# A hybrid attention layer on one core: four transfers a unit for sixteen, a product on VectorE, and other step counts

## The chip, the cores and the metric

The kernel runs on one core of a Trainium2 chip. The metric is the device time of one execution in microseconds. One execution is profiled, and the times below are those of its trace. The engines are TensorE (PE in the profile, and PEld for its weight loads), VectorE (DVE), ScalarE (ACT), GpSimd (POOL) and SyncE (SP), which issues the transfers.

## What is computed

One layer over 512 positions of width 1024 with two token mixers that read the same input: an attention of three branches (A) and a gated linear recurrence (B). Cut to what matters here:

```python
h = x @ w_in + b_in
(q_a, kv_a, g_nsa, z_a, q_b, f_b, i_b, z_b, gm_a, gm_b) = split(h)
# A: 8 heads in 2 groups of 4, width 64
o_cmp = masked_softmax(q @ kc.T) @ vc              # compressed keys and values
o_slc = masked_softmax(rope(q) @ rope(k_slc).T) @ v_slc
o_win = masked_softmax(rope(q) @ rope(k_win).T) @ v_win
o_a = (gt[0] * o_cmp + gt[1] * o_slc + gt[2] * o_win) * silu(z_a)
# B: recurrence over chunks of 64
o_b = hgrn2(q_b, f_b, i_b, lb)
o_b = o_b * rsqrt(mean(square(o_b)) + eps) * norm_g * silu(z_b)
y = sigmoid(gm_a) * (o_a @ w_branch_a) + sigmoid(gm_b) * (o_b @ w_branch_b)
out = layer_norm(alpha * x + y @ w_out)
```

With 512 positions the selected blocks and the window both cover all that comes before a position, so these two branches are causal attention with keys and values of their own.

## The kernel before

Everything is kept in SBUF with channels on the 128 partitions and positions along the row, up to the last stage. A product in float32 is done as three products of a high and a low part: `split2` casts the high part on ACT (L170) and subtracts it on DVE for the low part (L171). So each tile that goes into TensorE waits for a cast and then for a subtraction.

**What sets the order.** TensorE and the queue SP run what the program says in its order. The backbone is a row of projections: `proj(name)` does one 128-column tile of the input projection, 24 matmuls into one of two PSUM buffers `pa`; it loads the weights of the tile three further on and splits those of the tile two further on (`wraw`, `whi`, `wlo`, three buffers each). Into these projections other work is woven. A chain is a generator; every six matmuls of a projection (every second `kt`) make one tick (`weave.tick`, L82-94), at which each chain that is due runs on to its next `yield`. The number it yields is how many ticks it then rests. These numbers stand in the table `D` (L70-71): a chain `keys` that yields `D["r0"]` goes on r0 ticks later. A chain's instructions go into the queues of the engines at the tick at which it runs, so `D` sets what stands ahead of what on every engine.

**The chains.** `keys` and `queries` (r0) turn a projected tile by position and split it; `kh`, `kl` hold the keys of both branches. `cmp_kv` (c1, c2, c3) makes the compressed keys and values `kcB`, `vcB`, from a hidden tile that TensorE transposes into `hT`; `cmp_scores` and `cmp_probs` (p0, p1, p2) their softmax. `hgrn` (h0 to h6) is the recurrence, `hgrn_norm` (n0, n1, n2) its norm and gate, which makes the tiles `ob`.

**The units.** The masked attention runs in six units, `(i, branches)`: the last block of 128 queries (i = 3) with branch 0, then with branch 1, then i = 2 with either, then i = 1 with both and i = 0 with both. `attn_scores` (v0 to v3, e0) issues the score products of a unit, four of its eight heads at a time, then the masked reads with the row's minimum on DVE (L676) and the exponentials on ACT (L679). `soften` (e1, t0, t3, t1) scales the rows with gate and sum (L700 on ACT, L702 on DVE), and then turns the blocks: DVE transposes blocks of 32x32 into the one buffer `big` (L710), and transfers on SP bring these to their partitions in the one buffer `turn` (L719-721). After t1 ticks `values` splits the turned blocks (high part `t4<-turn` on ACT, low part in place on DVE) and after t2 more multiplies them with the values `vv` into two PSUM buffers `pso`. Since `turn` is one buffer, the next unit's transfers wait for this unit's values, and the next unit's transposes into `big` wait for this unit's transfers. With a query block's last product the sums go into `asum` (L747 on ACT, L751, L752 on DVE).

`attn_sum` (a5) adds the compressed branch, and when all four query blocks are there, multiplies with the gate (L781) and splits the four tiles `oa`.

**The end.** Eight groups of branch projections follow, four for mixer B with `ob` and then four for mixer A with `oa` (`BRANCH`, L922-950). Ahead of the first group of A, all chains are run to their end (`weave.drain`). Each group loads weights `wbr` three groups ahead, and output weights `wout` whose mean is taken out (L884, L886, L898, L899). A group's result is gated (L942), added to mixer B's (L946) and split, the tiles `y`. At the end come the output product and the norm by rows.

Of the kernel before, what the change touches and what calls it, by code (L numbers as in the profile page):

```python
# [13 lines left out]
ALU = mybir.AluOpType  # L14
# [6 lines left out]
NEG = -1.0e30  # L21
# [28 lines left out]
def _columns(name):  # L50

    c = np.arange(_COLS[name], _COLS[name] + 128)
    if name[0] == "q" and name[1] != "b" or name[:2] == "za":
# [12 lines left out]
K_ID, K_TRI, K_CM, K_RV, K_SM, K_COS, K_SIN, K_MASK, K_END = (  # L66
    0, 128, 256, 384, 388, 900, 1412, 1924, 2436)


D = dict(h0=6, h2=4, h3=7, h4=0, h5=5, h6=3, n0=6, n1=7, n2=4, c0=1, c1=5, c2=5, c3=4, r0=5, p0=5, p1=5, p2=2, s0=8,  # L70
         s2=5, s3=0, v0=10, v1=8, v2=7, v3=8, e0=4, e1=3, t0=6, t1=5, t2=4, t3=5, t4=1, a5=0)


class _Weave:
# [32 lines left out]
def layer_kernel(ctx: ExitStack, tc: tile.TileContext, xT, xn, w0, wi, wf, wv, small, brow, consts,  # L107
                 w1, w2, wbr, wout, lng, lnb, out):
    nc = tc.nc
    V, A, G = nc.vector, nc.scalar, nc.gpsimd  # L110
# [10 lines left out]
    def dma(o, i):  # L121
        tc.keep_in_program_order(nc.sync.dma_start(o, i))  # L122
# [3 lines left out]
    t2 = ctx.enter_context(tc.tile_pool(name="t2", bufs=57))  # L126
    t4 = ctx.enter_context(tc.tile_pool(name="t4", bufs=3))
# [8 lines left out]
    def T2(n=512, dt=F32):  # L136
        return t2.tile([P, n], dt, name="t2", tag="t2")
# [7 lines left out]
    def TURN():  # L145
        return turn.tile([P, 4096], F32R, name="turn", tag="turn")
# [7 lines left out]
    def PS():  # L154
        return pss.tile([P, 512], F32, name="pss", tag="pss")
# [4 lines left out]
    def PO():  # L160
        return pso.tile([P, 512], F32, name="pso", tag="pso")
# [4 lines left out]
    def act_set(name):  # L166
        return tc.keep_in_program_order(A.preload_act_table_set(name)).ins

    def split2(src, dst_hi, dst_lo):
        A.copy(dst_hi, src)  # L170
        V.tensor_tensor(dst_lo, src, dst_hi.bitcast(F32), ALU.subtract)  # L171
# [18 lines left out]
    for kt in range(KT):  # L190
# [6 lines left out]
        h, l, wh, wl = T2(dt=F32R), T2(dt=F32R), T2(dt=F32R), T2(dt=F32R)  # L197
# [160 lines left out]
    def chunks(ap):  # L358
        return ap.rearrange("p (t c s) -> p t c s", c=2, s=64)
# [28 lines left out]
    def hgrn(h):  # L388
# [11 lines left out]
        for w, e in ((1, e2), (0, e1)):  # L400
            V.tensor_tensor(chunks(e), cm[:, w].unsqueeze(3).to_broadcast([P, 4, 2, 64]), bc, ALU.subtract)
        yield D["h2"]
        qp = T2()
# [8 lines left out]
        V.tensor_tensor(e2, e2, k, ALU.mult)  # L412
        yield D["h3"]
        V.tensor_tensor(e1, e1, k, ALU.mult)
# [7 lines left out]
        V.tensor_tensor(qmc[:, :, 1], qpc[:, :, 1], ebc[:, :, 0, 63:64].to_broadcast([P, 4, 64]), ALU.mult)  # L422
        yield D["h4"]
        kMT = T2()
# [3 lines left out]
        for t in range(4):  # L428
# [4 lines left out]
                          pst_.rearrange("p (t s) -> p t s", s=128))  # L433
        yield D["h5"]
        while len(vi) < 4:
# [8 lines left out]
        for t in (1, 2):  # L444
            c = slice(128 * t, 128 * t + 128)
            V.scalar_tensor_tensor(st[:, c], st[:, 128 * t - 128:128 * t], dlab[:, t:t + 1], pu[:, c],
                                   ALU.mult, ALU.add)
        yield D["h6"]
        po = PO()
# [12 lines left out]
    def hgrn_norm():  # L462
        while len(osq) < 4:
            yield 1
        yield D["n0"]
        pm = PS()
        for h in range(4):
            T.matmul(pm[32 * h:32 * h + 32], ones, osq[h][1], start=True, stop=True)
        rs = T2()
        V.tensor_scalar(rs, pm, EPS, None, ALU.add)  # L470
        yield D["n1"]
        nat = act_set("natural_log_exp_and_others")
        with tc.issue_after(nat):
            A.activation(rs, rs, AF.Ln)
            A.activation(rs, rs, AF.Exp, scale=-0.5)
        exps.append(act_set("exp_and_others"))
        rms = []
        for h in range(4):
            rms.append(T2())
            for b in range(4):  # L480
                dma(rms[h][32 * b:32 * b + 32], rs[32 * h:32 * h + 32])
            yield 3
        yield D["n2"] - 9
        for h in range(4):
            while "zb%d" % h not in zs:
                yield 1
            o = osq[h][0]
            G.tensor_tensor(o, o, rms[h], ALU.mult)
            yield 2
            V.scalar_tensor_tensor(o, o, ngh[:, h:h + 1], zs["zb%d" % h], ALU.mult, ALU.mult)  # L490
            ob[h] = T2(dt=F32R), T2(dt=F32R)
            split2(o, *ob[h])
            yield 1
# [72 lines left out]
    def rope(raw):  # L566
        rot, r = T2(), T2()
        for b in range(4):
            dma(rot[32 * b:32 * b + 32], raw[32 * (b ^ 1):32 * (b ^ 1) + 32])
        V.tensor_tensor(r, raw, cosT, ALU.mult)  # L570
        return r, rot

    KH = cst.tile([P, 2, 512], F32R, name="kh")
    KL = cst.tile([P, 2, 512], F32R, name="kl")

    def keys(br, raw):
        r, rot = rope(raw)
        yield D["r0"]
        V.tensor_tensor(rot, rot, sinT, ALU.mult)
        V.tensor_tensor(r, r, rot, ALU.add)  # L580
        split2(r, KH[:, br], KL[:, br])
        ready.add("keys%d" % br)

    QAB = {}
# [60 lines left out]
    def attn_scores():  # L645
        blocks.append(BIG())
        for u, (i, brs) in enumerate(units):
            n, nb = 128 * (i + 1), len(brs)
            for ms in ((0, 1, 2, 3),) if i == 0 else ((0, 1), (2, 3)):
# [31 lines left out]

                weave.late.append(masked)
                weave.start(soften(u, ms, ts, den), D["e1"])
                yield D["v%d" % i]

    def soften(u, ms, ts, den):
        i, brs = units[u]
        n, nb, nm = 128 * (i + 1), len(brs), len(ms)
        while "gates" not in ready:
            yield 1  # L690
        V.reciprocal(den, den)
        den4 = den.rearrange("p (g m b) -> p g m b", g=2, m=nm)
        gate = gv[:, i, :, 1 + brs[0]:1 + brs[0] + nb].rearrange("p (g m) b -> p g m b", g=2)
        V.tensor_tensor(den4, den4, gate[:, :, ms[0]:ms[0] + nm], ALU.mult)  # L694
        for ab in range(2):
            for z, m in enumerate(ms):
                for x in range(nb):
                    c, h = slice(n * x, n * x + n), (ab * nm + z) * nb + x
                    if z % 2:
                        A.mul(ts[m, ab][:, c], ts[m, ab][:, c], den[:, h:h + 1])  # L700
                    else:
                        V.tensor_scalar(ts[m, ab][:, c], ts[m, ab][:, c], den[:, h:h + 1], None, ALU.mult)  # L702
        yield D["t0"]
        while turned[0] < u:
            yield 1
        nst = nb * (i + 1)
        view = blocks[0][:, 0:1024 * nst].rearrange("p (b c h s) -> p c b h s", b=4, h=8, s=32)
        for ab in range(2):
            for m in ms:
                V.transpose(view[:, :, :, 4 * ab + m],  # L710
                            ts[m, ab][:, 0:128 * nst].rearrange("p (c b s) -> p c b s", b=4, s=32))
        if ms[-1] == 3:
            yield D["t3"]
            while spent[0] < u:
                yield 1
            w = TURN()
            to = w.bitcast(F32)[:, 0:1024 * nst].rearrange("p (a x) -> p a x", a=4)
            of = blocks[0][:, 0:1024 * nst].rearrange("p (b x) -> p b x", b=4)
            for a in range(4):  # L719
                for b in range(4):  # L720
                    dma(to[32 * b:32 * b + 32, a], of[32 * a:32 * a + 32, b])
            turned[0] = u + 1
            yield D["t1"]
            for st in range(nst):
                part = w[:, 0:1024 * nst].rearrange("p (a c x) -> p c a x", a=4, x=256)[:, st]
                weave.start(values(u, st, part), D["t4"] * st)
# [111 lines left out]
    for name in SEQ:  # L838
# [5 lines left out]
        if name[0] == "k":  # L844
            weave.start(keys(int(name == "kwin"), evac(name)))
            continue
# [77 lines left out]
    for n, (mix, m0) in enumerate(BRANCH):  # L924
# [6 lines left out]
        for m in (m0, m0 + 1):  # L931
            ps = (PA, PS)[m % 2]()
            for kt in range(4):
# [3 lines left out]
                c = slice(512 * (m - m0) + 128 * kt, 512 * (m - m0) + 128 * kt + 128)  # L937
# [3 lines left out]
            r = T2()  # L941
# [93 lines left out]
def _constants():  # L1035
    c = np.zeros((128, K_END), np.float32)
    p = np.arange(128)
    c[:, K_ID:K_ID + 128] = np.eye(128)
    c[:, K_TRI:K_TRI + 128] = p[:, None] <= p[None, :]
    n = np.arange(32)  # L1040
    for i in range(4):
        t = 128 * i + p
        c[:, K_CM + 32 * i:K_CM + 32 * i + 32] = np.where(
            (16 * n[None, :] + 31 <= t[:, None]) & (n[None, :] < 31), 0.0, NEG)
        c[:, K_RV + i] = t >= 31
    c[:, K_SM:K_SM + 512] = np.arange(512) % 64 != 0
    inv = (np.float32(10000.0) ** (-np.arange(0, 64, 2, dtype=np.float32) / np.float32(64))).astype(np.float32)
    ang = np.arange(512, dtype=np.float32)[None, :] * inv[p % 32][:, None]
    c[:, K_COS:K_COS + 512] = np.cos(ang)
    c[:, K_SIN:K_SIN + 512] = np.sin(ang) * np.where(p % 64 < 32, -1.0, 1.0)[:, None]  # L1050
    c[:, K_MASK + 384:K_MASK + 512] = np.where(p[None, :] <= p[:, None], 0.0, NEG)
    return c


# [59 lines left out]
```

## Time and profile before

| | us |
|---|---|
| three runs | 427.97, 425.5, 426.37 |
| median | 426.37 |
| profiled execution, its own time | 427.06 |
| its span in the trace | 425.2 |
| mean granted TensorE clock | 0.994 |

The three runs differ by 2.5 us. The span goes from the first to the last instruction in the trace; 1.86 us of the execution's own time lie around it. In the rows of the profile, `pa`, `pss`, `pst` and `pso` are PSUM buffers, `t` is any of the general tiles of 128x512, and `L115` is the line of every matmul. The transfers by kind (size of one, and the median time from issue to landing) are, from the page's part on DMA issues:

```profile
wraw<-in_wf_dram SPq DMA_DIRECT2D x38, 512.0 KB, 3.6
turn<-big SPq DMA_DIRECT2D x48, 128.0 KB, 2.4
wraw<-in_wbr_dram SPq DMA_DIRECT2D x8, 512.0 KB, 6.0
turn<-big SPq DMA_DIRECT2D x32, 96.0 KB, 2.2
turn<-big SPq DMA_DIRECT2D x16, 64.0 KB, 2.0
```

The turned blocks are 48 + 32 + 16 transfers, 16 for each of six units: 2 MB for three of the units, 1.5 MB for two and 1 MB for the last.

### The profile page before, as it was taken

What the parts mean: (1) busy time and instruction counts of PE and PEld (TensorE: products, weight loads), DVE (VectorE), ACT (ScalarE), POOL (GpSimd) and SP (SyncE); (2) the same over time, 40 slices, a digit from 0 to 9 for tenths busy, and PEclk for the clock granted to TensorE, in tenths of its full rate; (3) what the DMA queues carried; (4) which work ended last, traced back from release to release, by engine and by line L of the source; (5) the groups of instructions that cost most, each with busy time, mean ns of one, the idle gap of its engine ahead of it and who ended that gap; (6) DMA issues with size and microseconds to landing.
All of it is one profiled execution on the core that took longest, in us unless ns stands there. A gap on an engine that the chain in (4) does not pass through costs nothing.

```text
span 425.2 us, 5979 instructions
## 1 busy us (share of the span) xinstructions
PE 409.8 (96%) x2063; PEld 334.2 (79%) x2063; DVE 314.8 (74%) x636; ACT 239.2 (56%) x469; POOL 10.1 (2%) x22
## 2 busy tenths in 40 slices
PE   9999999999999999979999999999999978999994
PEld 8888888889978687757887787788878856887884
DVE  5925698977485979987699679489766699774493
ACT  4535653544476635783667676578584776528301
POOL 2000000000010220000000000000000000000000
PEclk9999999999999999989999999999999999999999
DMA  7995300324113564804821542723944843026022
GB/s 263 396 387 174 137 0 22 130 76 143 57 49 106 170 202 109 256 2 131 206 109 50 132 168 77 190 81 99 230 167 101 293 142 107 0 72 226 2 100 98
DMA packets 25630, 58.05 MB, mean 137 GB/s; under 512 B 4480, under 2 KB 6400, under 8 KB 25600
## 3 DMA queue, kind: packets, MB, share of 16 engines
q1 hardware_dynamic: 25168, 57.28, 43.1%
q10 hardware_dynamic: 432, 0.39, 0.3%
q8 instruction: 16, 0.26, 0.3%
q14 instruction: 14, 0.11, 0.1%
HBM read 41.93 MB, written 2.10 MB: 104 GB/s over the span
## 4 chain that ended last, share of the span: by engine, by line
PE 78%; DVE 8%; ACT 5%; SPq 4%; DMA 2%; issue 2%; DVEq 0%; ACTq 0%
PE pa L115 51%; PE pso L115 12%; PE pss L115 12%; SPq L122 4%; PE pst L115 2%; DMA wraw<-in_wbr_dram 1%; DVE t L171 1%; DVE big L710 1%; ACT t L170 1%; DVE t L942 1%; DVE wlo L171 1%; ACT whi L170 1%; PE pst L119 1%; ACT t L679 1%; DVE t L899 1%
## 5 line engine op out<-in xcount | busy, mean ns | idle before, releaser
L115 PE MATMUL pa<-t,whi 128*128 128x512 f32 x640 | 201.5, 395 | 4.4 <-DVE t L171 3.0
L115 PEld LDWEIGHTS pa<-t,whi 128*128 128x128 f32 x640 | 118.6, 189 | 34.6 <-DVE t L171 4.3
L115 PE MATMUL pa<-t,wlo 128*128 128x512 f32 x320 | 125.0, 391 | 0.0
L171 DVE TENSOR_TENSOR wlo<-wraw,whi 128x1024 fp32r<-128x1024 f32 x46 | 56.7, 1234 | 23.7 <-ACT whi L170 23.6
L115 PEld LDWEIGHTS pa<-t,wlo 128*128 128x128 f32 x320 | 60.2, 188 | 12.8
L170 ACT CAST whi<-wraw 128x1024 fp32r<-128x1024 f32 x46 | 48.1, 1045 | 30.5 <-PE pa L115 24.1
L679 ACT ACTIVATE t<-t,sm_mn 128x512 f32<-128x512 f32 (+3 forms) x64 | 35.2, 551 | 27.6 <-DVE sm_mn L676 27.6
L115 PE MATMUL pso<-t,t 128*128 128x512 f32 (+2 forms) x158 | 32.8, 342 | 0.0
L115 PE MATMUL pss<-t,t 128*128 128x512 f32 (+2 forms) x158 | 30.6, 324 | 0.0
L171 DVE TENSOR_TENSOR turn<-turn,t 128x1024 fp32r<-128x1024 f32 x20 | 23.6, 1215 | 7.3 <-ACT t L170 7.2
L115 PEld LDWEIGHTS pso<-t,t 128*128 128x128 f32 x158 | 25.2, 189 | 3.7
L115 PE MATMUL pa<-t,t 128*128 128x512 f32 (+1 forms) x104 | 27.2, 366 | 0.0
L710 DVE STREAM_TRANSPOSE big<-t 128x512 f32<-128x512 f32 (+2 forms) x48 | 25.8, 590 | 1.0 <-PE pss L115 1.0
L115 PEld LDWEIGHTS pss<-t,t 128*128 128x128 f32 x158 | 24.0, 190 | 2.9
L170 ACT CAST t<-turn 128x1024 fp32r<-128x1024 f32 x20 | 20.0, 1048 | 3.8 <-DMA turn<-big 3.4
L115 PEld LDWEIGHTS pa<-t,t 128*128 128x128 f32 x104 | 18.3, 188 | 3.1
L170 ACT CAST t<-t 128x512 fp32r<-128x512 f32 (+1 forms) x18 | 10.6, 595 | 17.5 <-DVE t L946 12.7
L115 PE MATMUL pa<-turn,t 128*128 128x512 f32 x64 | 19.9, 389 | 0.0
L115 PE MATMUL pss<-t,whi 128*128 128x512 f32 x64 | 19.8, 390 | 0.0
L115 PE MATMUL pso<-t,vv 128*128 128x512 f32 x40 | 16.8, 421 | 2.1 <-ACT t L170 2.1
L700 ACT ACTIVATE t<-t,sm_dn 128x512 f32<-128x512 f32 (+3 forms) x32 | 16.0, 555 | 3.6 <-DVE sm_dn L694 3.5
L676 DVE CUSTOM_DVE_ANT_0 t<-pss,t 128x512 f32<-128x512 f32 (+3 forms) x32 | 14.0, 483 | 5.2 <-PE pss L115 5.2
(198 smaller groups left out, 569.9 us busy)
## 6 DMA issues: line engine op xcount, KB each, us to landing
wraw<-in_wf_dram SPq DMA_DIRECT2D x38, 512.0 KB, 3.6
turn<-big SPq DMA_DIRECT2D x48, 128.0 KB, 2.4
wraw<-in_wbr_dram SPq DMA_DIRECT2D x8, 512.0 KB, 6.0
t<-in_wout_dram SPq DMA_DIRECT2D x16, 256.0 KB, 4.5
t<-t SPq DMA_DIRECT2D x48, 64.0 KB, 2.0
turn<-big SPq DMA_DIRECT2D x32, 96.0 KB, 2.2
t<-in_wi_dram SPq DMA_DIRECT2D x8, 256.0 KB, 6.0
big<-in_w_dram SPq DMA_DIRECT2D x8, 256.0 KB, 5.7
```

Of the source, the lines that this page charges most:

```text
L115: return tc.keep_in_program_order(nc.tensor.matmul(*a, **k))
L119: return tc.keep_in_program_order(nc.tensor.transpose(*a, **k))
L122: tc.keep_in_program_order(nc.sync.dma_start(o, i))
L170: A.copy(dst_hi, src)
L171: V.tensor_tensor(dst_lo, src, dst_hi.bitcast(F32), ALU.subtract)
L676: V.tensor_tensor_reduce(out=p[:, c], in0=dsts[m, ab][:, c], in1=amask[:, 512 - n:512], op0=ALU.add, op1=ALU.min, scale=-0.125, scalar=3.0e38,
L679: A.activation(p[:, c], p[:, c], AF.Exp, bias=mn[:, h:h + 1], scale=-1.0, accum_out=den[:, h:h + 1])
L700: A.mul(ts[m, ab][:, c], ts[m, ab][:, c], den[:, h:h + 1])
L710: V.transpose(view[:, :, :, 4 * ab + m], ts[m, ab][:, 0:128 * nst].rearrange("p (c b s) -> p c b s", b=4, s=32))
L899: V.scalar_tensor_tensor(lo, raw, nm, hi.bitcast(F32), ALU.add, ALU.subtract)
L942: V.scalar_tensor_tensor(r, gm["g%s%d" % (mix, m)], 1.0, ps, ALU.add, ALU.mult)
```

## The change

Four things are edited.

1. The keys of a block of 128 are put in another order: position 4r + b (r below 32, b below 4) goes to place 32b + r. `keys` does it in its split, which reads the turned tile with a step of four and writes evenly. The causal mask of the diagonal block (a constant) is written for the same order.
2. After the 32x32 transposes, one set of 32 partitions of `big` holds, for each r, the four keys 4r to 4r + 3. So one transfer a set can write them to the partitions 4r + b, all 128 of them: four transfers a unit, each from 32 partitions to 128, where sixteen went from 32 partitions to 32. The bytes are the same, and the values keep their order.
3. In `hgrn_norm` the product of a tile with its norm is on VectorE instead of GpSimd, and the rest of two ticks behind it is gone.
4. Sixteen numbers of `D` are others.

```diff
-D = dict(h0=6, h2=4, h3=7, h4=0, h5=5, h6=3, n0=6, n1=7, n2=4, c0=1, c1=5, c2=5, c3=4, r0=5, p0=5, p1=5, p2=2, s0=8,
-         s2=5, s3=0, v0=10, v1=8, v2=7, v3=8, e0=4, e1=3, t0=6, t1=5, t2=4, t3=5, t4=1, a5=0)
+D = dict(h0=6, h2=4, h3=7, h4=0, h5=7, h6=4, n0=7, n1=7, n2=0, c0=1, c1=5, c2=4, c3=1, r0=7, p0=3, p1=9, p2=2, s0=8,
+         s2=9, s3=0, v0=13, v1=6, v2=7, v3=8, e0=5, e1=5, t0=6, t1=5, t2=3, t3=5, t4=1, a5=4)
@@ hgrn_norm
-            G.tensor_tensor(o, o, rms[h], ALU.mult)
-            yield 2
+            V.tensor_tensor(o, o, rms[h], ALU.mult)
@@ ahead of keys
+    def turned_keys(ap, form):
+        return ap.rearrange(form, b=4, r=32)
@@ keys
-        split2(r, KH[:, br], KL[:, br])
+        split2(turned_keys(r, "p (c r b) -> p c b r"), turned_keys(KH[:, br], "p (c b r) -> p c b r"),
+               turned_keys(KL[:, br], "p (c b r) -> p c b r"))
@@ soften
             for a in range(4):
-                for b in range(4):
-                    dma(to[32 * b:32 * b + 32, a], of[32 * a:32 * a + 32, b])
+                dma(to[:, a], of[32 * a:32 * a + 32])
@@ _constants
-    c[:, K_MASK + 384:K_MASK + 512] = np.where(p[None, :] <= p[:, None], 0.0, NEG)
+    key = 4 * (p % 32) + p // 32
+    c[:, K_MASK + 384:K_MASK + 512] = np.where(key[None, :] <= p[:, None], 0.0, NEG)
```

Lines behind `keys` have numbers higher by two or three in the changed kernel (L710 is L713 there, L676 is L679, L866 is L868), those between `hgrn_norm` and `keys` lower by one (L551 is L550).

How this moves instructions shows on three engines. First VectorE, at the first unit: `big` takes the last transposes (the second four heads), `wlo` is a low part of weights, and the L676 (now L679) are the masked reads of the next unit's first four heads. Before:

```order
L532 RECIPROCAL t2_1647<-t2_1647 128x128
L710 STREAM_TRANSPOSE big_1278<-t2_1512 128x4x4x32
L533 TENSOR_TENSOR t2_1648<-pss_1608,t2_1647 128x128
L710 STREAM_TRANSPOSE big_1278<-t2_1509 128x4x4x32
L710 STREAM_TRANSPOSE big_1278<-t2_1515 128x4x4x32
L867 SCALAR_TENSOR_TENSOR t2_1669<-t2_1670,t2_1669 128x512
L171 TENSOR_TENSOR wlo_1677<-wraw_1590,whi_1676 128x1024
L171 TENSOR_TENSOR t2_1696<-t2_960,t2_1695 128x512
L676 ISA t2_1717,sm_mn_1699<-pss_1701,t2_325 128x512
```

The same place after:

```order
L713 STREAM_TRANSPOSE big_1265<-t2_1537 128x4x4x32
L713 STREAM_TRANSPOSE big_1265<-t2_1534 128x4x4x32
L869 SCALAR_TENSOR_TENSOR t2_1660<-t2_1661,t2_1660 128x512
L679 ISA t2_1707,sm_mn_1689<-pss_1691,t2_325 128x512
L679 ISA sm_mn_1689 128x1
L679 ISA t2_1710,sm_mn_1689<-pss_1692,t2_325 128x512
L679 ISA sm_mn_1689 128x1
L679 ISA t2_1713,sm_mn_1689<-pst_1699,t2_325 128x512
L679 ISA sm_mn_1689 128x1
L679 ISA t2_1716,sm_mn_1689<-pst_1700,t2_325 128x512
L679 ISA sm_mn_1689 128x1
L713 STREAM_TRANSPOSE big_1265<-t2_1540 128x4x4x32
```

The last transpose, on which the unit's transfers wait, has moved behind the four masked reads. Next ScalarE, where the first unit's turned blocks are cast: `t4<-turn` are these casts, `vcB` a copy of the compressed values, and L679 (now L682) the exponentials of the second unit's second four heads. Before:

```order
L679 ACTIVATE t2_1866,sm_dn_1843<-t2_1866,sm_mn_1842 128x512
L679 ACTIVATE t2_1869,sm_dn_1843<-t2_1869,sm_mn_1842 128x512
L679 ACTIVATE t2_1872,sm_dn_1843<-t2_1872,sm_mn_1842 128x512
L679 ACTIVATE t2_1875,sm_dn_1843<-t2_1875,sm_mn_1842 128x512
L170 CAST t2_1885<-t2_1229 128x512
L700 ACTIVATE t2_1872<-t2_1872,sm_dn_1843 128x512
L864 ACTIVATE t2_1902<-pa_1823,sml_105 128x512
L866 ACTIVATE t2_1903<-pa_1823,hbias_333 128x512
L700 ACTIVATE t2_1875<-t2_1875,sm_dn_1843 128x512
L551 COPY vcB_348<-pst_1935 128x128
L170 CAST t4_1860<-turn_1754 128x1024
L170 CAST t4_1863<-turn_1754 128x1024
```

After:

```order
L170 CAST whi_1807<-wraw_1740 128x1024
L550 COPY vcB_348<-pst_1829 128x128
L170 CAST t2_1814<-t2_1310 128x512
L170 CAST t4_1912<-turn_1818 128x1024
L170 CAST t4_1915<-turn_1818 128x1024
L170 CAST t4_1924<-turn_1818 128x1024
L682 ACTIVATE t2_1866,sm_dn_1849<-t2_1866,sm_mn_1848 128x512
L682 ACTIVATE t2_1869,sm_dn_1849<-t2_1869,sm_mn_1848 128x512
L682 ACTIVATE t2_1872,sm_dn_1849<-t2_1872,sm_mn_1848 128x512
L682 ACTIVATE t2_1875,sm_dn_1849<-t2_1875,sm_mn_1848 128x512
```

The casts stood behind the exponentials, and three of them now stand ahead. Last the queue SP, where the last unit's transfers stand among the loads of branch weights (`wraw`) and output weights (`t2`). Before:

```order
L122 DMA wraw_3118<-in_wbr_dram 128x1024
L122 DMA t2_3168<-in_wout_dram 128x512
L122 DMA t2_3169<-in_wout_dram 128x512
L122 DMA wraw_3177<-in_wbr_dram 128x1024
L122 DMA turn_3201<-big_1278 32x512 x16
L122 DMA t2_3238<-in_wout_dram 128x512
L122 DMA t2_3239<-in_wout_dram 128x512
L122 DMA wraw_3259<-in_wbr_dram 128x1024
```

After:

```order
L122 DMA wraw_3061<-in_wbr_dram 128x1024
L122 DMA turn_3111<-big_1265 128x1x512 x4
L122 DMA t2_3124<-in_wout_dram 128x512
L122 DMA t2_3125<-in_wout_dram 128x512
L122 DMA wraw_3133<-in_wbr_dram 128x1024
L122 DMA t2_3166<-in_wout_dram 128x512
L122 DMA t2_3167<-in_wout_dram 128x512
L122 DMA wraw_3187<-in_wbr_dram 128x1024
```

The unit's transfers come one group of branch weights earlier, and are four.

## The prediction

> **What bounds the kernel now.** I read the page's head first, then the clock and DMA share of some stretches, then TensorE's own timeline wherever it shows a wait, and last the engine and queue that each wait names.
>
> ```profile
> span 425.2 us, 5979 instructions
> PE 409.8 (96%) x2063; PEld 334.2 (79%) x2063; DVE 314.8 (74%) x636; ACT 239.2 (56%) x469; POOL 10.1 (2%) x22
> ```
>
> TensorE is busy for 409.8 of 425.2 us, and the change adds or removes no matmul. So only the 15.4 idle us, and stretches at a low clock, can be won; every further wait of TensorE is lost in full. The stretches (columns: window, length, busy time of PE, PEld, DVE, ACT, POOL, granted clock, DMA share, GB/s):
>
> ```profile
> 3.00:20.00 17.00, 17.00 (x88) 14.70 (x88) 15.32 (x35) 7.27 (x11) 0.00 (x0) 1.00 1.01 367
> 165.00:176.00 11.00, 11.00 (x53) 8.79 (x50) 10.33 (x22) 8.72 (x17) 0.00 (x0) 1.00 0.89 199
> 188.40:191.80 3.40, 3.40 (x9) 2.58 (x9) 3.40 (x5) 1.97 (x3) 0.00 (x0) 0.50 0.00 0
> 318.00:329.30 11.30, 11.30 (x52) 9.32 (x51) 7.45 (x10) 5.89 (x11) 0.00 (x0) 1.00 0.39 93
> ```
>
> 52 matmuls in 11.30 us are .217 us each; that is my step below. At clock .50 nine took 3.40 us: 3.40 - 9 x .217 = 1.45 us lost there. TensorE's waits that this change can reach are these (start, duration, in brackets the idle time before and its releaser):
>
> ```profile
> 141.17 0.39 PE L115 MATMUL pst<-kl,t 64*128 64x512 f32 x2
> 142.55 0.50 PE L115 MATMUL pst<-kh,t 64*128 64x512 f32 x2 [0.99 <-DVE t L171]
> ...
> 183.79 0.78 PE L115 MATMUL pst<-t,t 128*128 128x64 f32 x6
> 186.64 0.51 PE L115 MATMUL pso<-t,vv 128*128 128x512 f32 x1 [2.07 <-ACT t L170]
> 187.90 0.50 PE L115 MATMUL pso<-turn,vv 128*128 128x512 f32 x1 [0.75 <-DVE turn L171]
> ...
> 346.74 0.39 PE L115 MATMUL pss<-t,wlo 128*128 128x512 f32 x1
> 348.50 0.70 PE L115 MATMUL pa<-t,whi 128*128 128x512 f32 x2 [1.38 <-DVE t L942]
> 350.88 0.50 PE L115 MATMUL pa<-t,whi 128*128 128x512 f32 x1 [1.21 <-DVE t L171]
> 352.08 0.50 PE L115 MATMUL pa<-t,whi 128*128 128x512 f32 x1 [0.24 <-DVE t L171]
> 354.60 0.50 PE L115 MATMUL pa<-t,whi 128*128 128x512 f32 x1 [1.56 <-DVE t L171]
> ...
> 384.62 1.23 PE L115 MATMUL pst<-t,t 128*128 128x512 f32 x3 [0.68 <-ACT t L170]
> ```
>
> Four places: the last query's low part at 142.55, the first unit's values at 186.64, the hand-over to the a-branches at 348.5 to 354.6, and the last y tile at 384.62. A matmul after a wait also takes .50 in place of .39, so each wait costs some .1 more than its bracket. Behind the waits stand these rows of the queue SP, of ACT, DVE and POOL:
>
> ```profile
> 164.30 10.05 SPq L122 DMA_DIRECT2D turn<-big  x16
> 318.04 10.01 SPq L122 DMA_DIRECT2D turn<-big  x16
> 328.09 1.08 SPq L122 DMA_DIRECT2D t<-in_wout_dram  x2
> 329.27 0.38 SPq L122 DMA_DIRECT2D wraw<-in_wbr_dram  x1
> ```
>
> ```profile
> 185.54 2.94 ACT L170 CAST t<-turn 128x1024 fp32r<-128x1024 f32 x3
> 335.67 1.05 ACT L170 CAST whi<-wraw 128x1024 fp32r<-128x1024 f32 x1 [2.25 <-DMA wraw<-in_wbr_dram]
> 338.59 1.19 ACT L747 COPY t<-pso 64x512 f32<-64x512 f32 x2
> ```
>
> ```profile
> 171.85 2.09 DMA turn<-big
> ```
>
> ```profile
> 329.27 6.32 DMA wraw<-in_wbr_dram
> ```
>
> The last two are pieces of the chain that ended last. The first unit's 16 transfers are issued from 164.30 to 174.35; with 2.09 us to land, the data are there by 176.4, but ACT casts them only at 185.54. So the first unit waits for the order on ACT, not for its transfer. The last unit's 16 issues hold SP for 10.01 us; the weight load behind them is issued at 329.27, lands at 335.6, and ACT stands 2.25 us for it with the copy of the finished sums (L747) queued behind. DVE is then late for the four oa tiles: the waits at 348.5 to 354.6.
>
> **The transfers themselves.** Sixteen issues take 10.05 us, .63 each. Four, bounded by this row from below (.63 each) and from above (four times as long each, since each now carries four blocks): 2.5 to 10 us. I take 2.5, since the 512 KB weight load was issued in .38 us, below the .63 of a 128 KB turned one: bytes don't set it. The rate: for a 2 MB unit the DMA engines are .89 busy at 199 GB/s, so the engines and not the issues set it, and 2 MB take 10.5 us. Bounds for four transfers from 32 partitions to 128: 367 GB/s as in the loads of 3 to 20 us (5.7 us), and half of 199 (21 us). I take 199, the row of the same SBUF-to-SBUF bytes. Then a 2 MB unit wins nothing; the last unit (1 MB) ran at 93 GB/s and .39 share, held by its issues, and would take 5.3 in place of 10 us. [...]
>
> **First unit's values (moved by t2, v0, s2, n2).** Before, ACT reached the three casts only after the next score group's exponentials, a vcB copy and a weight cast. Now they stand ahead of that group's exponentials, and TensorE comes to the products 26 matmuls later in the program (883 before it then, 909 now): 26 x .217 = 5.6 us, of which the waits removed ahead take some. On the other side the last DVE transpose now stands behind the four masked reads, so the transfer starts near 167.6 instead of 164.3 and lands near 179.3 (167.6 + 10.5 + about 1). TensorE comes to it near 188.5; cast and low part need 2.3 of the 9 us between, so the cover is some 6. I count the 2.07 + .75 + two restarts of .1 and the 1.45 of low clock as gone, but for .2 at a later low part: +4.3 (bounds 0, if ACT is still late, and 4.5). Next late is the exponentials of the second group, which now stand behind the casts.
>
> **Hand-over (moved by e1, v1; four issues).** The last unit's values stand 18 matmuls earlier in the program (1551 matmuls before them, 1569 then), 3.9 us, its four issues give SP back 7.5 us early, and the unit is issued one weight load earlier, so that no load stands behind it that ACT needs at once. The wait chain 1.38 + 1.21 + .24 + 1.56 and four restarts are 4.8; DVE still has as much work between the sums and the last oa tile as TensorE has matmuls, so I leave .2: +4.6 (bounds +1, if DVE only shifts, and 4.8).
>
> **Product of the norm, from POOL to DVE.** These rows bear on it:
>
> ```profile
> 140.66 1.28 POOL L488 TENSOR_TENSOR t<-t,t 128x512 f32<-128x512 f32 x1 [20.42 <-DMA t<-t]
> ...
> 154.15 1.70 POOL L488 TENSOR_TENSOR t<-t,t 128x512 f32<-128x512 f32 x1 [6.45 <-DMA t<-t]
> ```
>
> ```profile
> 140.72 1.77 DVE L171 TENSOR_TENSOR t<-t,t 128x512 fp32r<-128x512 f32 x1
> 144.25 2.17 DVE L510 TENSOR_TENSOR t<-t,sml 128x496 f32<-128x496 f32 x2
> 154.63 1.77 DVE L867 SCALAR_TENSOR_TENSOR t<-t,t 128x512 f32<-128x512 f32 x1
> 164.19 0.65 DVE L867 SCALAR_TENSOR_TENSOR t<-t,t 128x512 f32<-128x512 f32 x1
> 182.58 0.68 DVE L171 TENSOR_TENSOR t<-t,t 128x512 fp32r<-128x512 f32 x1
> ```
>
> While POOL multiplies, DVE's own instruction is stretched: L171 1.77 for .68, L867 1.77 for .65, some 1.1 each. DVE pays four new products of about .68 = 2.7 us and gets back up to four stretches of .6 to 1.1: about nothing in DVE's time. The first stretch is what TensorE waited for at 142.55. But there the two L510 adds (L509 now; 2.17 us) now stand ahead of the same low part, and they wait for a transfer. I leave a wait of .7 of the 1.1: +.4 (bounds -1.5 and +1.1).
>
> **Where new waits come.** c3 goes from 4 to 1: 12 matmuls now stand between the turned hidden tile and its product, 2.6 us, and DVE has two copies to make in that time behind some 10 us of queued reads, products and casts: -.8 (bounds 0 and -1.5). Second unit: its casts stand ahead of ga0's tanh on ACT, and TensorE needs that PSUM buffer; laying the new order out with the durations of the rows before, I put the landing at 210.7, the tanh at 218.8 and TensorE's need of the buffer at 217.1, estimates all three: -1.7 (bounds 0 and -3). In the a-branches DVE's chain of a tile runs with the lag seen at the end:
>
> ```profile
> 381.90 0.69 DVE L171 TENSOR_TENSOR t<-t,t 128x512 fp32r<-128x512 f32 x1 [0.69 <-ACT t L170]
> 384.60 0.69 DVE L171 TENSOR_TENSOR t<-t,t 128x512 fp32r<-128x512 f32 x1 [0.68 <-ACT t L170]
> ```
>
> One tile takes 2.70 us there, more than its 12 matmuls (2.6). TensorE used to wait for oa ahead of these and gave DVE time; without those waits I take 1.4 for the .7 before: -.7 (bounds 0 and -1.5). The split of the keys through a reordered view is strided; nearest are the L510 rows, 1.09 against .68 for an even read: up to .4 twice on DVE and ACT, at 0, covered by the e0 and r0 ticks before the first scores; without that cover -.8. The mask constant costs nothing: same bytes, same reads. The other numbers of the table move chains within TensorE's full stretches (third to fifth unit), where I find no wait before and none after: 0, between -1 and +1.
>
> **Sum.** 4.3 + 4.6 + .4 - .8 - 1.7 - .7 = 6.1 us. The profiled execution's own time is 427.06 us (span 425.2), so 421.0; the median of the runs, 426.37, lies .69 lower: 420.3. What a measurement of this kernel can tell from no change is .5%, 2.1 us.
>
> **Rivals.** A, the forecast: 420.3, its own range 416 to 424.
> B, the transfers become slower. Sixteen DMA engines read 32 partitions at a time; if they crowd on fewer of these than before, 2 MB take 21 in place of 10.5 us. The first unit then lands near 190, some 10 us of wait; the second again some 10, the fifth some 5: +25, less the 6.1, and about 440 (436 to 446). It turns from gain to loss once 2 MB take some 5 us more: the second unit has no cover left and loses all of it, the first has some 6. For it speaks that the engines already are .89 busy at a little over half of the loads' 367 GB/s; against it, that the bytes and source partitions are the same.
> [...]
> C, the waits only move: all four new ones at their bounds (-1.5, -3, -1.5, and -1.5 at the last query) against 4.3 + 4.6: +1.4, 425. For it: TensorE has 96%, and DVE 74%.
> D, the transfers reach the loads' 367 GB/s, and none of the new waits come: 4.5 + 4.8 + 1.1 + .7 = 11.1, 415. Against it: 32 source partitions remain.
>
> **Chances.** A .56, B .17, C .15, D .12. The range 414.5 to 427.5 holds A, C and D whole, .83; B is left out. Faster by over .5% (under 424.2): A nearly whole, D, some of C: .68. Same: C's rest and A's end, .15. Slower: B, .17.
>
> **What would show it.** The SP row of a unit: four issues in some 2.5 us, and the time from the last issue to landing. TensorE's waits for L170 at the first unit and L171 at the hand-over gone, no stretch at clock .50 near 188. New waits named DVE hT copies (L538), ACT L920 and L171 at y7, .7 to 1.7 each. Wrong would be a wait of several us whose releaser is a cast of turn, with the transfer landing late (B), or an ACT that waits for turn with ready work queued behind it.

## The result: slower, 430.9 us for 426

| | before | changed |
|---|---|---|
| median of the runs, us | 425.94 (4 runs) | 430.85 (4 runs, 430.45 to 431.38) |
| profiled execution, us | 427.06 | 431.38 |
| ratio, 95% interval | | 1.0107 (1.0070 to 1.0143) |

I had forecast 420.3 in a range of 414.5 to 427.5. The page of the changed kernel, its head and the transfers by kind (size of one, median time to landing):

```profile
span 429.6 us, 5863 instructions
PE 412.3 (96%) x2063; PEld 336.0 (78%) x2063; DVE 312.9 (73%) x640; ACT 239.4 (56%) x469; POOL 4.9 (1%) x18
...
turn<-big SPq DMA_DIRECT2D x12, 512.0 KB, 9.0
turn<-big SPq DMA_DIRECT2D x8, 384.0 KB, 6.9
```

TensorE's own timeline, at the places where it waits now:

```profile
146.45 0.51 PE L115 MATMUL pst<-kh,t 64*128 64x512 f32 x2 [1.39 <-DVE t L171]
...
191.45 0.73 PE L115 MATMUL pa<-t,whi 128*128 128x512 f32 x2 [1.91 <-ACT t L868]
...
224.45 1.13 PE L115 MATMUL pa<-t,whi 128*128 128x512 f32 x2 [2.73 <-ACT t L920]
...
292.28 0.50 PE L115 MATMUL pso<-turn,vv 128*128 128x512 f32 x1 [2.00 <-DVE turn L171]
...
317.13 0.50 PE L115 MATMUL pso<-turn,vv 128*128 128x512 f32 x1 [0.71 <-DVE turn L171]
...
359.18 0.50 PE L115 MATMUL pa<-t,whi 128*128 128x512 f32 x1 [1.22 <-DVE t L171]
```

Behind two of these waits TensorE runs at half clock (window, length, busy time of PE, PEld, DVE, ACT, POOL, granted clock, DMA share, GB/s); at .217 us a matmul, 1.2 and 1.3 us are lost there (3.40 less ten matmuls, 3.30 less nine):

```profile
224.60:228.00 3.40, 3.40 (x10) 2.38 (x12) 3.40 (x7) 1.57 (x3) 0.00 (x0) 0.50 0.44 154
292.90:296.20 3.30, 3.30 (x9) 2.59 (x8) 2.85 (x8) 3.30 (x12) 0.00 (x0) 0.50 0.00 0
```

What ACT and DVE did ahead of these waits: SP's row of the first unit's four transfers, the casts on ACT for the first two units, and the DVE transposes that wait for `big`:

```profile
169.61 7.79 SPq L122 DMA_DIRECT2D turn<-big  x4
```

```profile
184.47 2.94 ACT L170 CAST t<-turn 128x1024 fp32r<-128x1024 f32 x3 [4.54 <-DMA turn<-big]
187.32 0.72 ACT L682 ACTIVATE t<-t,sm_mn 128x512 f32<-128x512 f32 x1
...
190.73 0.68 ACT L868 ACTIVATE t<-pa,hbias 128x512 f32<-128x512 f32 x1
...
217.00 2.94 ACT L170 CAST t<-turn 128x1024 fp32r<-128x1024 f32 x3 [6.20 <-DMA turn<-big]
...
223.71 0.68 ACT L920 ACTIVATE t<-pa,hbias 128x512 f32<-128x512 f32 x1
```

```profile
184.50 0.71 DVE L713 STREAM_TRANSPOSE big<-t 128x512 f32<-128x512 f32 x1 [3.48 <-DMA turn<-big]
...
217.03 0.58 DVE L713 STREAM_TRANSPOSE big<-t 128x384 f32<-128x384 f32 x1 [4.33 <-DMA turn<-big]
...
279.16 2.49 DVE L713 STREAM_TRANSPOSE big<-t 128x512 f32<-128x512 f32 x4 [3.54 <-DMA turn<-big]
```

Each unit's casts stand in ACT's queue ahead of work that empties TensorE's PSUM buffers (L868, L920). The casts wait for a transfer that has not landed, and what stands behind them is held up with them. In all, the two engines wait for transfers of `turn` and `big` as follows; first before (two kinds of waits: total, times, longest), then after:

```profile
ACT t L170 <- DMA turn<-big: 3.4, 1, 3.4
```

```profile
ACT t L170 <- DMA turn<-big: 21.9, 5, 6.2
DVE big L713 <- DMA turn<-big: 24.1, 5, 9.2
```

By the trace's landing records, from a unit's first issue to its last landing, in us:

| unit (MB) | 1 (2) | 2 (2) | 3 (1.5) | 4 (1.5) | 5 (2) | 6 (1) |
|---|---|---|---|---|---|---|
| before, sixteen | 11.9 | 12.8 | 12.2 | 11.6 | 11.9 | 11.4 |
| changed, four | 14.8 | 14.2 | 10.4 | 11.3 | 14.8 | 7.5 |

Four transfers are slower for 2 MB and quicker for less.

### The profile page after: what moved, and what is told of

Its sections match the earlier page's. It is cut to its first block, busy times and chain, and to the rows that moved or that the text cites. A ratio compares the mean times of both kernels' runs of the same rounds, so it can differ in the third digit from the quotient of the medians.

```text
span 429.6 us, 5863 instructions
## 1 busy us (share of the span) xinstructions
PE 412.3 (96%) x2063; PEld 336.0 (78%) x2063; DVE 312.9 (73%) x640; ACT 239.4 (56%) x469; POOL 4.9 (1%) x18
## 4 chain that ended last, share of the span: by engine, by line
PE 59%; DVE 15%; DMA 12%; SPq 6%; ACT 5%; issue 2%; DVEq 0%; ACTq 0%
PE pa L115 34%; PE pso L115 11%; PE pss L115 10%; DMA turn<-big 8%; SPq L122 6%; PE pst L115 4%; DVE wlo L171 3%; DVE big L713 3%; DMA wraw<-in_wf_dram 2%; ACT t L170 2%; DMA wraw<-in_wbr_dram 2%; DVE turn L171 1%; DVE t L901 1%; ACT t L682 1%; DVE t L171 1%
## 5 line engine op out<-in xcount | busy, mean ns | idle before, releaser
L171 DVE TENSOR_TENSOR wlo<-wraw,whi 128x1024 fp32r<-128x1024 f32 x46 | 55.8, 1218 | 17.4 <-ACT whi L170 17.1
L682 ACT ACTIVATE t<-t,sm_mn 128x512 f32<-128x512 f32 (+3 forms) x64 | 35.1, 551 | 19.5 <-DVE sm_mn L679 19.5
L713 DVE STREAM_TRANSPOSE big<-t 128x512 f32<-128x512 f32 (+2 forms) x48 | 26.5, 595 | 26.1 <-DMA turn<-big 24.1
L170 ACT CAST t<-turn 128x1024 fp32r<-128x1024 f32 x20 | 20.0, 1047 | 22.3 <-DMA turn<-big 21.9
L115 PE MATMUL pss<-t,whi 128*128 128x512 f32 x64 | 19.7, 390 | 0.0
L115 PE MATMUL pso<-turn,vv 128*128 128x512 f32 x40 | 16.4, 410 | 2.7 <-DVE turn L171 2.7
```

Of the source, the lines that this page charges most:

```text
L115: return tc.keep_in_program_order(nc.tensor.matmul(*a, **k))
L682: A.activation(p[:, c], p[:, c], AF.Exp, bias=mn[:, h:h + 1], scale=-1.0, accum_out=den[:, h:h + 1])
L713: V.transpose(view[:, :, :, 4 * ab + m], ts[m, ab][:, 0:128 * nst].rearrange("p (c b s) -> p c b s", b=4, s=32))
```

## The experiments

I had two theories at first: the longer 2 MB transfers cost (theory 1 in the texts below, S later on), or the counts cost by themselves (theory 2). Four runs took the parts asunder.

**New counts and product, sixteen transfers, old keys.** The part on the transfers, against the changed kernel; the split of the keys and the mask go back with it:

```diff
-                dma(to[:, a], of[32 * a:32 * a + 32])
+                for b in range(4):
+                    dma(to[32 * b:32 * b + 32, a], of[32 * a:32 * a + 32, b])
```

> The new counts and the product on VectorE, with sixteen transfers a unit and the old key order. In the changed kernel a 2 MB unit took 14.3 to 14.9 us from first issue to landing (three units), before 11.6 to 12; the last one took 7.5 in place of some 11.5. Theory 1 (the longer transfers): ACT and TensorE no longer wait for the first, second and fifth unit, so waits of 1.9, 2.9 with its stretch at half clock (1.45) and 0.9 shrink, some 5 us back, less up to 4 lost again at the hand-over to the a-branches: 425 to 428. Theory 2 (the counts by themselves set the casts and transposes in the way, whatever a transfer takes): 430 to 433, with the waits at the second and fourth unit still there.

Measured 443.09 (ratio 1.0389, 1.0353 to 1.0426). Outside both. ACT waits only 2.7 us for transfers here; TensorE waits 11.9 us for casts and low parts of the turned blocks. The first unit has landed at 181.0, and TensorE waits 2.9 us for its values up to 194.0: in this run the casts stand late, not early.

**Four transfers and new keys alone**: the kernel before with the diff's parts in `keys`, `soften` and the mask, and nothing else.

> The kernel before with four transfers a unit and the new key order alone: old counts, product on GpSimd. Both theories, if the long transfers are covered by the old order (the first unit's cast then came 9 us after its landing): faster by what the last unit wins at the hand-over, 4 us, so 421 to 424. If a 2 MB transfer of 14.5 us costs with the old counts too (theory 1 in its strong form): 426 to 430, with a new wait for a cast of turn.

Measured 442.51 (1.0381, 1.0338 to 1.0424). That is more than even the strong form of theory 1 (426 to 430).

**The changed kernel with the product on POOL.**

```diff
-            V.tensor_tensor(o, o, rms[h], ALU.mult)
+            G.tensor_tensor(o, o, rms[h], ALU.mult)
+            yield 2
```

> The changed kernel with the norm's product back on GpSimd and its rest of two ticks. Theory 1 and 2: the product is not what costs, 430 to 432. Rival 3 (four more products on VectorE, a dense engine there, delay the transposes and low parts of the first unit): 427 to 429, and the wait of 1.78 us at 144.7 gone or the first unit's transfer issued 1 to 3 us earlier.

Measured 431.06 (1.0096, 1.0069 to 1.0123) beside the changed kernel's 430.85: with the new counts the product's engine is worth nothing that shows.

**The changed kernel with the old table `D`.**

> The changed kernel with the old table of counts: four transfers, new key order, product on VectorE. Theory 2 (counts): like the run with four transfers alone, 420 to 424. Theory 1 in its strong form: 427 to 431. Against the run with four transfers alone it shows the product's price by itself, which I expect between -1 and +1 us.

Measured 446.49 (1.0462, 1.0434 to 1.0490). So new counts with old transfers lose 17 us, and old counts with new transfers 16, or 20 with the product on VectorE; only together are they within 5. Neither theory says that. From the run with four transfers alone this one differs by the product and its rest, and by 4 us where I expected at most 1. The order of ACT and DVE differs between the two as well, so this is not the price of the product by itself. ACT's waits for transfers in the run with four transfers alone:

```profile
ACT t L170 <- DMA turn<-big: 27.9, 5, 7.3
```

The order of the instructions told why. In that run TensorE's order is that of the kernel before, row for row; but on ACT 322 and on DVE 366 lines differ, though no count was touched. So what I wrote of `D`, that it sets what stands ahead of what on every engine, does not hold for ACT and DVE. These two are ordered when the kernel is built. I read it so that they are ordered by when operands are expected, and that four transfers are expected sooner than sixteen; no run here shows why the order came out so. Part of the comparison on ACT at the first unit (- before, + four transfers; `t<-t,sm_mn` are the exponentials):

```
-CAST t<-t 128x512
-ACTIVATE t,sm_dn<-t,sm_mn 128x512
...
+CAST t<-turn 128x1024
+ACTIVATE t<-pa,sml 128x512
+ACTIVATE t<-pa,hbias 128x512
+CAST whi<-wraw 128x1024
+CAST t<-t 128x512
+CAST t<-turn 128x1024
+CAST t<-turn 128x1024
+ACTIVATE t,sm_dn<-t,sm_mn 128x512
```

This made theory O: the order counts on a landing that comes later on the chip. What the order costs can be put to the test, since it can be held: the next kernels add to each instruction on ACT, DVE and POOL an edge to the one that stands ahead of it in another kernel.

```diff
+        for one, then in zip(order, order[1:]):
+            tc.add_manual_dep(then, one.name, mybir.DependencyInfo(
+                mybir.DependencyClass.NoSync, mybir.DependencyReason.DATA), reason="pin")
```

**Four transfers, old counts, in the order of the kernel before.**

> The kernel before with four transfers a unit and the new key order (old counts, product on GpSimd), and with the queues of ACT, DVE and POOL held, instruction by instruction, in the order that they have in the kernel before. With four transfers alone, the order on TensorE was unchanged, and yet 322 rows of the comparison on ACT and 366 on DVE differed: the planner that lays out these two queues when the kernel is built put the casts of turn earlier. Theory O (the order made for quicker transfers than the chip's is what costs): the 16 us of that run vanish, and the last unit, landing 4 us earlier, still helps: 421 to 425, ACT's wait for turn under 3 us in all (27.9 there). Theory S (the 2 MB transfers of 14.3 to 14.9 us cost by themselves): 430 to 442.

Measured 423.80 (0.9929, 0.9907 to 0.9951). As O said; ACT waits for no transfer of `turn` at all, and the hand-over's 4.4 us of waits are 0.44:

```profile
351.33 0.50 PE L115 MATMUL pa<-t,whi 128*128 128x512 f32 x1 [0.44 <-DVE t L171]
```

**Sixteen transfers, old counts, in the order of the run with four.**

> The kernel before, with its sixteen transfers, old keys and old counts, and with ACT, DVE and POOL held in the order that they have in the run with four transfers and old counts. Theory O: the order costs with the old transfers too, since these land no sooner than 11.6 to 12 us: 436 to 444. Theory S: with transfers 3 us quicker for the three 2 MB units the loss is mostly gone: under 431.

Measured 444.35 (1.0422, 1.0378 to 1.0466). The order alone costs 18 us, with the old transfers too. S falls for this pair.

**The changed kernel in the order of the first run (new counts, sixteen transfers).**

> The changed kernel, all its parts, with ACT, DVE and POOL in the order that they have in the run with new counts and sixteen transfers (443.1). Theory O: the order and the counts together set it, and the casts of turn stand late there against TensorE's products: 438 to 446, near that run. If the changed kernel's own order is what loses (it puts the casts ahead of the landing), a later order should help: under 428.

Measured 437.13 (1.0248, 1.0207 to 1.0289), a little under the range. With order and counts alike, four transfers are 6 us better than sixteen (443.09).

**New counts, sixteen transfers, in the order of the changed kernel.**

> The changed kernel with only the transfers undone: sixteen a unit, old key order, new counts, product on VectorE, and ACT, DVE and POOL held in the order of the changed kernel. The 2 MB units land after 11.6 to 12 us instead of 14.3 to 14.9, the 1.5 MB units some 1 us later than there, the last some 4 us later. Theory S: the waits of 1.9, of 2.9 with 1.45 at half clock, and of 0.9 go, the hand-over loses up to 4: 424 to 428. Theory O in its strong form (the order assumes a landing far earlier than either): 429 to 434.

Measured 433.34 (1.0124, 1.0066 to 1.0182; its runs went from 429.7 to 437.4). Its 2 MB units land after 12.0 to 12.2, but the third unit after 11.8 (10.4 in the changed kernel) and the last after 11.4 (7.5), and ACT still waits 19.7 us for them. Sixteen transfers don't fit that order either. S, which had 424 to 428, falls here too: quicker 2 MB transfers alone do not mend this order.

**One cast moved, with four transfers in the order of the kernel before**: the first unit's first cast on ACT and its low part on DVE go one group ahead.

> Four transfers, old counts, product on GpSimd, ACT and DVE in the order of the kernel before (423.8), with two instructions moved in that order: the first cast of the first unit's turned blocks ahead of the cast that follows the second unit's exponentials, and its subtraction on DVE ahead of that cast's. In the run without the move the unit had landed at 179.7 and TensorE waited 1.9 and 1.1 us for these two at 185 to 188, with a stretch at half clock behind (1.45). Theory O: order alone makes these waits: 419 to 421.5. Rival: what is pushed back (gate tiles, copies) makes TensorE wait as long elsewhere: 423 to 425.

Measured 423.88 (0.9922, 0.9891 to 0.9953), no change. The rival's price was right and its place not: the first product has no wait now, and the second turned block, whose cast was not moved, has it:

```profile
184.49 0.48 PE L115 MATMUL pso<-t,vv 128*128 128x512 f32 x1
...
187.45 0.50 PE L115 MATMUL pso<-t,vv 128*128 128x512 f32 x1 [1.78 <-ACT t L170]
```

**The changed kernel, nine instructions moved**: in the first two units, three casts each go behind what stood ready behind them, and a transpose behind the masked reads; in the fourth unit, one low part goes forward. ACT's order at the first unit:

```diff
-CAST t<-turn (three)
 ACTIVATE t,sm_dn<-t,sm_mn (four)
+CAST t<-turn (three)
 ACTIVATE t<-pa,sml
```

> The changed kernel in its own order but for nine moves: in the first two units the casts of turn on ACT go behind the exponentials (second unit: behind ga0's tanh too) and the one DVE transpose that waits for the transfer goes behind the masked reads; in the fourth unit the second low part goes ahead of the masked reads. Theory O (the changed kernel loses since its order puts these ahead of the landing, and ready work stands behind them): the waits of 1.9, 2.7 and 2.0 us and two stretches at half clock (1.45 each) go: 422 to 426. Rival (the new counts lose by themselves: TensorE comes to the products too soon): 428 to 432.

Measured 421.95 (0.9884, 0.9860 to 0.9909): 9 us better than the changed kernel, with the same transfers and counts. ACT's wait is down from 21.9 to 12.0, and TensorE's largest are these:

```profile
PE pso L115 <- DVE turn L171: 2.1, 2, 1.1
PE pst L115 <- DVE t L171: 1.4, 1, 1.4
```

Why do four transfers land later? The next pair has eight transfers a unit and differs only in their source partitions: 16 neighbours, or every second one of 32. Both are in the order of the changed kernel. The second leaves keys at places that the mask does not fit, and serves for its time alone.

```diff
-                dma(to[64 * h:64 * h + 64, a], of[32 * a + 16 * h:32 * a + 16 * h + 16])
+                dma(to[64 * h:64 * h + 64, a], of[32 * a + h:32 * a + 32:2])
```

> The changed kernel with eight transfers a unit, each from 16 neighbouring partitions to 64, ACT and DVE in its order. [...] Rival N (only the number of transfers and their issue count): 12 to 13.

> As the run with eight halves, but each transfer reads every second partition of the 32 (even, then odd), to the same 64 destinations: bytes, number and sizes are the same and only the source partitions differ, so that keys go to other places and the output is not the layer's. [...] Rival N: as with halves, within .5 us.

Measured, one run each: 434.16 with halves, 422.67 with every second. SP's row of the first unit, halves and then every second, and the pages' rows of the transfers, halves and then every second:

```profile
169.05 10.64 SPq L122 DMA_DIRECT2D turn<-big  x8
```

```profile
169.80 8.48 SPq L122 DMA_DIRECT2D turn<-big  x8
```

```profile
turn<-big SPq DMA_DIRECT2D x24, 256.0 KB, 5.6
```

```profile
turn<-big SPq DMA_DIRECT2D x24, 256.0 KB, 4.9
```

The 2 MB units landed after 15.0, 14.6 and 15.0 us with halves, 12.1 three times with every second. Number, size and destinations are the same, so it is the choice of source partitions. With that choice it also changes which source goes to which destination; the pair does not part the two.

**The same with the right keys**, in the order of the changed kernel: position 64h + 4i + b goes to place 32b + 2i + h, and the split is made for each h.

> The changed kernel in its own order of ACT and DVE, with eight transfers a unit that each read every second of 32 partitions, and the keys and the mask put in the order that goes with it (the split of the keys is two instructions on ACT and two on DVE in place of one, twice). Theory P (the loss comes from transfers that crowd on neighbouring source partitions, against an order that counts on a sooner landing): a 2 MB unit lands after 12 to 12.3 us, and the time is 421 to 424, as in the one look with keys at other places (422.7). Rival: that one look was chance, or the right split of the keys costs what the transfers win: 426 to 431.

Measured 422.37 (0.9912, 0.9883 to 0.9941). Its units land after 12.2, 12.3, 9.3, 10.1, 12.1 and 6.9 us, each sooner than in the changed kernel. The run with sixteen transfers in this order (433.34) has its 2 MB units as soon, but its smaller ones after 11.4 to 11.8.

**Both remedies together.**

> The run with even and odd partitions and the right keys, with the nine moves in the order of ACT and DVE that brought the changed kernel to 421.95. If both remedies take away the same waits (theory O: landing against order, one cause): little more than either alone, 419 to 423. If they were two causes, their gains of 9 us would add: 413 to 416.

Measured 419.09 (0.9823, 0.9790 to 0.9856), the fastest. The remedies alone won 8.9 and 8.5 us on the changed kernel, together 11.8: mostly one cause, reached from two sides. ACT's waits for transfers are 5.6 us:

```profile
ACT t L170 <- DMA turn<-big: 5.6, 2, 2.9
```

## Why the prediction was wrong

The step that failed is the transfer's: "I take 199, the row of the same SBUF-to-SBUF bytes". Four transfers moved the 2 MB in 14.2 to 14.8 us where I had 11.5. They were also issued later than I had them, the first unit's at 169.61 for 167.6. Both together put its landing at 184.4 and not at 179.3, and the second unit's at 216.9 and not at 210.7. Rival B was right in its direction: in the pair of runs the transfers from neighbouring source partitions are slower (14.6 to 15.0 us for 12.1). Its 21 us for 2 MB, at half the rate, no run shows: 2.1 MB in 14.6 us is 144 GB/s with the landing in it, where 21 us would be 100.

The trace shows what is late. Each transfer lands in sixteen parts. In the 2 MB units the first and the last of these are some .3 us apart in the median before; with four transfers 2.1 to 2.6, and up to 4.4; with every second partition under 1. All in all the DMA engines moved 183 GB/s from 169.6 to 184.4, a piece of the next weight load among it, for 189 from 164.3 to 176.2 before: the sum is hardly slower, but the last part is. The packets agree: those of the 1.5 MB units, which can be told by their size, took 222 ns in the median before (5th to 95th percentile 128 to 248), and now 121 with a tail to some 520. So most are quicker and the slowest take longer; what holds those up was not shown.

The second failure made some 3 us decisive. For the first unit I wrote of a cover of "some 6", measured from the casts to TensorE's need of their product. That product had no wait, the late landing notwithstanding: in the traces it stands 34 matmuls later than before (1019 ahead of it for 985), not the 26 that I counted, and TensorE came to it at 192.95, not near 188.5. What had a wait was TensorE's next PSUM buffer, behind L868, which stood on ACT behind exponentials, which stood behind the casts. I had named these ("Next late is the exponentials") and priced them at 0. B put the turn from gain to loss at some 5 us more for 2 MB; here some 3 more went with a loss. B's price, 440, was still too dear, and its own terms, +25 less the 6.1, give 445.

Point by point, in TensorE's waits with the half clock:

| place | forecast | measured | from |
|---|---|---|---|
| first unit | +4.3 | +2.4 | 2.07 + .75 + 1.45 gone, 1.91 new |
| hand-over | +4.6 | +3.2 | 4.39 to 1.22 |
| last query's low part | +.4 | -.4 | .99 to 1.39 |
| hidden tile (c3) | -.8 | 0 | no wait there |
| second unit | -1.7 | -3.9 | 2.73, 1.2 at half clock |
| last y tile | -.7 | +.7 | .68 to none |
| fourth and fifth unit | 0 | -4.0 | 2.00, 1.3 at half clock, .71 |

The measured column sums to -2.0 of the -4.3 between the profiled executions; .8 more is lost in the first 8 us (TensorE's 41st matmul starts at 8.51, before at 7.74), and the rest is spread. The .8 belongs to the single execution: over all the profiled ones here that matmul starts between 7.73 and 9.01, and the latest is in a kernel faster than the one before (423.80). The second unit holds one half of the loss, where a 2 MB transfer came late, and the fourth the other. The hand-over was the right idea: it won in each run with four transfers in a fitting order, though the last unit's four issues held SP for 4.08 us and not 2.5. The last query's low part waited behind the two L509 adds, as I wrote, for 1.39 and not .7. That at 279.16 the transposes of the next unit wait 3.54 us for the fourth unit's transfer, and push its low part, I had not seen at all; that transfer is no slower than before (11.3 for 11.6), so the order makes this wait. A quicker transfer in the same order (10.1, every second partition) shortens TensorE's 2.00 there to .96 as well. Of the two pairs that exchange only the product, the one with the new counts shows nothing (431.06 for 430.85) and the one with the old counts 4 us, with another order on ACT and DVE; what the product costs by itself stays open.

What I did not know was the larger thing: counts, order and landing have to fit each other. An exchange of the counts or of the transfers alone, which changes the order with it, costs 16 to 20 us, and 18 where the order alone was exchanged. That the order was laid out for an expected landing is my reading of it.

Not tried: transfers that land as soon as the casts stand in the order, which would show whether the order is then without loss. A smaller transfer would leave parts of `turn` unwritten.

## What to carry to other kernels

A change to transfers can reorder engines that it does not touch (322 lines on ACT and 366 on DVE here): compare the order on every engine ahead of pricing anything, and hold the order when the transfer itself is to be measured. In an in-order queue, an instruction that waits for a transfer has as much cover as the most urgent one behind it, not as its own reader has: the first unit's product did not wait, and L868 behind its casts held TensorE for 1.91 us. And for transfers within SBUF, look at which partitions are read at once: in eight transfers to 64 partitions each, every second one of 32 landed 2 MB in 12.1 us where neighbours took 14.6 to 15.0.

## What the runs showed of the hardware

- Eight transfers of 256 KB from 16 neighbouring partitions land 2 MB in 14.6 to 15.0 us, and from every second one of 32 in 12.1, with the same destinations.
- With four transfers from 32 partitions to 128, the sixteen parts in which one transfer lands are 2.1 to 2.6 us apart in the median of a 2 MB unit, for .3 with sixteen transfers from 32 to 32.
- The granted clock falls to .50 for some 3.4 us a little after TensorE has waited: behind single waits of 2.00 and 2.73 us here, and behind 2.07 with .75 before; behind the one of 1.91 it stayed at 1.00. The length of the wait alone does not tell: with sixteen transfers in the order of the changed kernel it fell behind a wait of 1.58, and with eight halves it stayed at 1.00 behind one of 2.12.
- The issue of four transfers takes 7.79 us for 2 MB, not the 2.5 that I took: .65 and .60 for the first two, then 3.99 and 2.40. The issue goes with the transfer: eight issues took 10.64 us where 2 MB landed in 15.0, and 8.48 where they landed in 12.1.
